# The second mixer's stages in another order: stick-breaking first, the recurrence last

## Chip, cores and metric

One Trainium2 chip, one core. The metric is the device time of one launch in microseconds (us); a change of some 0.2% can be told from none.

## What is computed

Two transformer blocks follow each other on 512 tokens of width 1024, in fp32. The first has a hybrid mixer, cross attention and a feed-forward part; the second has two layers of feed-forward, **mixer**, feed-forward, each with a modulated norm. The change lies in that mixer alone, which runs twice:

```python
def _mixer(h, ...):
    (lru_x, lru_g, sb_q, sb_k, sb_v, fx_q, fx_k, fx_v, fx_f) = split(h @ w_in)
    u = causal_depthwise_conv(lru_x, conv_w, conv_b)
    y_lru = rg_lru(u, w_rgate, b_rgate, w_igate, b_igate, lru_lambda) * gelu(lru_g)
    y_sb = stick_breaking_attention(sb_q, sb_k, sb_v)
    fq, fk = rms(fx_q) * g_qk[0], rms(fx_k) * g_qk[1]
    log_f = log_sigmoid(fx_f + b_fgate)
    y_fox = forgetting_attention(fq, fk, fx_v, log_f)
    y = concat([rms(y_lru), rms(y_sb), rms(y_fox)]) * g_mix_out
    return y @ w_out
```

The recurrence `rg_lru` has two block-diagonal gates with a sigmoid, a decay `a = exp(log_a)`, a factor `sqrt(1 - a*a)` and a scan over the 512 tokens. The stick-breaking attention weighs a key by its own log-sigmoid plus a reversed running sum over later keys; the forgetting attention is a softmax with a decay from cumulated forget gates. Each has four heads of 64; the recurrence is 512 wide.

## The kernel before

**Tiles.** Activations are kept with features on the partitions, 128 x 512 tokens a tile. Every large product is made of three fp32r matmuls (`mm3`, L343: high x high, high x low, low x high), so each weight tile (128 x 1024, DMA on SP's queue, `weights` L329) is split by ACT (`wh`) and by DVE or POOL (`wl`). There are 3 raw, 6 high and 6 low weight buffers, 43 activation buffers ("a"), 12 rotating ones ("r"), 3 PSUM buffers "mm" for the large products and 5 "x" for all else.

**Order.** TensorE's order is written by hand. `Flow` (L209) keeps a planned time: the main generator yields the planned TensorE time of each product, and side streams (spawned with a delay) are run whenever their planned time has come, ahead of the main one. A side stream that must let another engine work yields `Wait`. The delays are the constants in `T` (L193): `lru_sum` 25.0, `rsqrt` 3.51, `fqk` 8.0, `fox` 1.0, `fox_1` 0.9, `fox_2` 0.41, `stick` 1.81, `stick_l` 4.0, `finish` 4.91. TensorE then executes in this fixed order and waits wherever an input is late. The other engines are ordered by the framework's scheduler, by program order among what is ready.

**The mixer** (`mixer2`, L1322), main stream in this order:

1. `dense_t` of eight feature tiles, the first five "ahead" in token halves while the norm before is still made: gelu branch `lgg` (4), then the convolved branch `lx` (4, four DVE operations each, L1336 and L1339).
2. `lru` (L1268) is spawned: eight gate matmuls `lg` (L1281) with weights `bd`, tanh, exp, sqrt on ACT, products on POOL, scans on DVE (L1305), times gelu, sum of squares; then the function table 6 (exp and ln) is loaded and, 25 planned us later, the norm (`spread`: column sums `ms`, inverse root, row broadcast `bc`) makes `HL`.
3. `dense_tok` of the forgetting queries and keys (`fqk`), normed per head and turned (`turn`, 8 us later, into `FT`).
4. `dense_t` of the forget gate, then `gates` (L1384): transposes, log-sigmoid, cumulated sums `cs`, four row broadcasts `fb`.
5. `dense_t` of the stick queries and keys (`sqk`).
6. The streams `stick(t)` and `fox(t)` for the four query blocks t = 0 to 3 of 128 tokens are spawned; `heads` (L993) chains the blocks of a kind. A stick needs all scores, Abs, Exp, Ln, a reversed scan, a POOL subtraction and an Exp before its transposes and products; a forgetting block runs its four heads through `pipeline` (L1062). Each block ends with `finish` (norm and turn into `YT`).
7. `dense_tok` of the values `v`, beside 6.
8. `slab4` with the first half of `w_out` on the recurrence's `HL` (96 matmuls), then `end_plain` with the second half on `YT`, by token halves, where `made` waits for the blocks of a half.

Of the kernel before, what the change touches and what calls it, by code (L numbers as in the profile page):

```python
# [19 lines left out]
S = 512  # L20
# [262 lines left out]
class Core:  # L283
# [706 lines left out]
        yield from self.end_post(I["w_out"][0], AT, Y, "post_mix_g", self.nxt1("pre_mem_g"), H2,  # L990
                                 self.rows_apart, lambda hf: _joined([halves[hf]]))

    def heads(self, makers, delay, opened=None):  # L993


        out = []

        def chain(i):
            if i and opened is None:
                yield from _joined([out[i - 1]])  # L1000
            elif i:
                yield from _joined(out[:i - 1])
                while i - 1 not in opened or opened[i - 1] > self.flow.t:
                    yield Wait(0.5)
            yield from makers[i]()
        for i in range(len(makers)):
            out.append(self.flow.spawn(chain(i), delay))
        return out
# [256 lines left out]
                                        op0=OP.mult)  # L1265
            self.a4.append(a4), self.hb.append(hb)

    def lru(self, l, LX, LG, HL):  # L1268

        nc, I = self.nc, self.I  # L1270
# [4 lines left out]
        U, R, G, sums = [], [], [], []  # L1275
        for m in range(4):
            u = LX[m]
            r, g = self.act("lr"), self.act("li")
            for q, o in enumerate((r, g)):
                ps = self.ps("x", "lg")  # L1280
                nc.tensor.matmul(ps, bd[q][:, m * 128:m * 128 + 128], u,  # L1281
                                 start=True, stop=True)
                nc.scalar.activation(o, ps, AF.Tanh, scale=0.5, bias=hb[:, q * 4 + m:q * 4 + m + 1])
                yield _pe(512)
            nc.vector.scalar_tensor_tensor(u, g, 1.0, u, op0=OP.add, op1=OP.mult)

            nc.scalar.activation(g, r, AF.Tanh, scale=a4[:, m:m + 1], bias=a4[:, m:m + 1])
            U.append(u), R.append(r), G.append(g)
        bd.clear()
        yield Wait(T["lru_tanh"])  # L1290
        for m in range(4):
            c = a4[:, 4 + m:5 + m]
            nc.scalar.activation(R[m], R[m], AF.Exp, scale=c, bias=c)
        for m in range(4):
            u, a, g = U[m], R[m], G[m]

            q = self.rot("a2")
            nc.gpsimd.tensor_tensor(q, a, a, op=OP.mult)
            nc.vector.scalar_tensor_tensor(g, q, 1.0, g, op0=OP.add, op1=OP.mult)
        for m in range(4):  # L1300
            u, a, g = U[m], R[m], G[m]
            nc.scalar.activation(g, g, AF.Sqrt, scale=0.25)
            nc.gpsimd.tensor_tensor(u, u, g, op=OP.mult)
            hs = self.rot("hs")
            nc.vector.tensor_tensor_scan(hs, a, u, 0.0, op0=OP.mult, op1=OP.add)  # L1305
            nc.vector.tensor_tensor(u, hs, LG[m], op=OP.mult)
            self.square_sum(sums, u, self.rot)

        self.table = self.load_table(6)
        yield Wait(T["lru_sum"])  # L1310
        out = []
        yield from self.spread(sums, 4, 1.0 / 512, out)
        for m in range(4):
            t = self.rot("ln")
            nc.vector.scalar_tensor_tensor(t, U[m], self.vec(f"g_mix{l}", m), out[0], op0=OP.mult,
                                           op1=OP.mult)
            hi, lo = self.act("lh", F32R), self.act("ll", F32R)
            nc.scalar.activation(hi, t, AF.Copy)
            nc.vector.tensor_tensor(lo, t, hi.bitcast(F32), op=OP.subtract)
            HL.append((hi, lo))  # L1320

    def mixer2(self, l, H, H2):  # L1322
        nc, I, flow = self.nc, self.I, self.flow
        LX, LG, Q, K, v = {}, {}, {}, {}, {}


        cw = lambda j, m: self.vec(f"conv_w{l}", j * 4 + m)

        def lru_in(i, ps):
            if i < 4:  # L1330
                LG[i] = self.act("lgg")
                nc.scalar.activation(LG[i], ps, AF.Gelu_apprx_tanh)
            else:
                i -= 4
                u = self.act("lx")
                nc.vector.tensor_scalar(u, ps, cw(3, i), self.vec(f"conv_b{l}", i), op0=OP.mult,  # L1336
                                        op1=OP.add)
                for d in (1, 2, 3):
                    nc.vector.scalar_tensor_tensor(u[:, d:], ps[:, :S - d], cw(3 - d, i), u[:, d:],  # L1339
                                                   op0=OP.mult, op1=OP.add)  # L1340
                LX[i] = u
        yield from self.dense_t([I["m_t"][l, i] for i in (4, 5, 6, 7, 0, 1, 2, 3)], H, lru_in, 5)
        HL, self.table, self.calm = [], None, False
        lru = flow.spawn(self.lru(l, LX, LG, HL), 1.0)


        fqk, FT, squares = {}, [], {}
# [1 line left out]
        def qk(t, ps):  # L1349
# [27 lines left out]
        fT = self.rot("fT")  # L1377

        def gate_in(i, ps):
            nc.scalar.activation(fT[:4], ps[:4], AF.Copy)  # L1380
        yield from self.dense_t([I["m_f"][l]], H, gate_in)
        NF, FB = self.tp.tile([128, 16], F32, tag="nf", bufs=1, name=self.nm("NF")), []

        def gates():  # L1384
# [30 lines left out]
                FB.append(o)  # L1415
                yield 4 * _pe(128)
        gated = flow.spawn(gates(), 1.0)

        def qk_stick(i, ps):
            d = self.act("sqk")  # L1420
            if i < 2:
                nc.scalar.activation(d, ps, AF.Copy, scale=0.125)
                Q[i] = d
            else:
                nc.vector.tensor_copy(d, ps)
                K[i - 2] = d
# [49 lines left out]
        def fox(t):  # L1476
# [10 lines left out]
            def score(h):  # L1487
                if h % 2 == 0:
                    scs[h], scs[h + 1] = scores(FT[:2], FT[2:], h // 2, t, self.mask["le"])
                sc = scs.pop(h)  # L1490
                e = es[h] = self.rot("fe")
                nc.vector.tensor_tensor_reduce(out=e[:, :n], in0=sc, in1=FB[h][:, :n], scale=1.0,
                                               scalar=-3.0e38, op0=OP.add, op1=OP.max,
                                               accum_out=m[:, h:h + 1])
                c = slice(h, h + 1)
                nc.vector.tensor_tensor(b[:, c], nf[:, c], m[:, c], op=OP.subtract)
                nc.vector.tensor_tensor(b[:, c], b[:, c], nf[:, c], op=OP.subtract)
                nc.scalar.activation(e[:, :n], e[:, :n], AF.Exp, bias=b[:, c],
                                     accum_out=lsum[:, c])
                return 0.0 if h % 2 else _pe(n) + 0.2  # L1500

            def second(h):
# [12 lines left out]
        def stick(t):  # L1515
# [52 lines left out]
        yield from self.dense_tok([I["m_v"][l, c] for c in range(4)], H, keep, e=nc.gpsimd)  # L1568
        H.clear()
# [12 lines left out]
        yield from self.end_plain(I["m_o"][l, 1], YT, gate, self.nxt2(l, 2), H2, made)  # L1582


    def program(self, stop):
# [77 lines left out]
```

## Time and profile before

| what | us |
|---|---|
| median of 3 runs | 2888.01 (2886.16 to 2888.03) |
| the profiled execution | 2887.57 |
| its span | 2885.5 |
| busy in it: TensorE / DVE / ACT / POOL | 2784.1 / 1534.0 / 1027.6 / 383.5 |
| mean granted TensorE clock | 0.98 |

All times in the rows are from one profiled execution. A TensorE that is busy is one with a matmul in it; the ends of matmuls are modelled, so the spacing of starts tells its rate better. In a row of waits the releaser is the engine, tile and line that came last. In a row of stretches the numbers in brackets are instructions.

### The profile page before, as it was taken

The page shows a single profiled execution, that of the slowest core. Times are in us where ns is not written, and L with a number is a line of the kernel's source. Part 1 is how long each engine was busy: PE and PEld are TensorE (multiplying, and loading weights), DVE is VectorE, ACT ScalarE, POOL GpSimd, SP SyncE. Part 2 cuts the span into 40 slices and gives each one's busy share as a digit, 9 for nine tenths or more (in the row PEclk, how much of TensorE's full clock was granted, in tenths as well). Part 3 has the DMA queues.
Part 4 walks back from the last instruction along what each step waited for, and adds up shares of the span by engine and source line. Part 5 has one row for each costly group of instructions (what it writes and reads, how often), then busy time and mean ns, then how long its engine had stood idle before and what let it go on. Part 6 is the DMA issues. An engine that isn't in the chain of part 4 may idle for free. (4 is left out here: it accounts for less than half of the span.)

```text
span 2885.5 us, 36900 instructions
## 1 busy us (share of the span) xinstructions
PE 2784.1 (96%) x14492; PEld 2355.3 (82%) x14492; DVE 1534.0 (53%) x2931; ACT 1027.6 (36%) x1725; POOL 383.5 (13%) x376
## 2 busy tenths in 40 slices
PE   8999998999989999998799999999999988999999
PEld 7888878888878888887588888888888875888888
DVE  6465666645456444466766454463333667643333
ACT  4355444323233222245543222342222535432221
POOL 3010303101032000024310000110000232200000
PEclk9999999999998999999999999999999997999999
DMA  5322322555433555431115555353332321133322
GB/s 164 121 69 88 103 88 74 168 160 169 148 114 123 160 169 161 139 116 54 52 52 162 156 174 159 112 173 110 102 95 88 95 62 34 52 98 93 102 90 71
DMA packets 94606, 326.07 MB, mean 113 GB/s; under 512 B 11232, under 2 KB 15584, under 8 KB 94432
## 3 DMA queue, kind: packets, MB, share of 16 engines
q1 hardware_dynamic: 94288, 323.53, 36.4%
q8 instruction: 114, 1.87, 0.3%
q14 instruction: 60, 0.49, 0.1%
q10 hardware_dynamic: 144, 0.18, 0.0%
HBM read 321.37 MB, written 2.10 MB: 112 GB/s over the span
## 5 line engine op out<-in xcount | busy, mean ns | idle before, releaser
L338 ACT ACTIVATE wh<-wr 128x1024 fp32r<-128x1024 f32 x456 | 482.3, 1060 | 1273.0 <-PE mm L347 494.8
L346 PE MATMUL mm<-hh,wh 128*128 128x512 f32 (+1 forms) x2344 | 856.9, 366 | 7.3 <-ACT fqk L1352 2.4
L348 PE MATMUL mm<-hh,wl 128*128 128x512 f32 (+1 forms) x2344 | 852.4, 364 | 3.0 <-DVE wl L340 3.0
L347 PE MATMUL mm<-hl,wh 128*128 128x512 f32 (+1 forms) x2344 | 852.9, 364 | 1.7 <-DVE hl L500 1.6
L340 DVE TENSOR_TENSOR wl<-wr,wh 128x1024 fp32r<-128x1024 f32 x440 | 541.8, 1233 | 343.1 <-ACT wh L338 341.2
L346 PEld LDWEIGHTS mm<-hh,wh 128*128 128x128 f32 x2344 | 448.4, 191 | 76.6 <-ACT fqk L1352 3.3
L348 PEld LDWEIGHTS mm<-hh,wl 128*128 128x128 f32 x2344 | 448.4, 191 | 71.2 <-DVE wl L340 3.6
L347 PEld LDWEIGHTS mm<-hl,wh 128*128 128x128 f32 x2344 | 448.2, 191 | 69.6 <-DVE hl L500 2.0
L795 DVE CUSTOM_DVE_ANT_0 ada<-ada,c 128x1024 f32<-128x1024 f32 x144 | 180.4, 1253 | 314.4 <-DMA ada<-in_w_ada_dram 314.2
L346 PE MATMUL dn<-uh,wh 128*128 128x512 f32 x720 | 280.1, 389 | 0.0
L347 PE MATMUL dn<-ul,wh 128*128 128x512 f32 x720 | 280.1, 389 | 0.0
L348 PE MATMUL dn<-uh,wl 128*128 128x512 f32 x720 | 280.1, 389 | 0.0
L490 POOL TENSOR_TENSOR acc<-sq,sq 128x256 f32<-128x256 f32 (+1 forms) x34 | 38.3, 1129 | 1377.2 <-ACT sq L487 1377.2
L633 DVE TENSOR_TENSOR sg<-mm,sg 128x512 f32<-128x512 f32 x110 | 75.9, 690 | 181.8 <-PE mm L348 177.4
L346 PE MATMUL mmt<-wh,hh 128*128 128x512 f32 x352 | 147.1, 418 | 12.1 <-ACT wh L338 8.2
L348 PEld LDWEIGHTS dn<-uh,wl 128*128 128x128 f32 x720 | 135.1, 188 | 28.1
L346 PEld LDWEIGHTS dn<-uh,wh 128*128 128x128 f32 x720 | 135.1, 188 | 28.1
L347 PEld LDWEIGHTS dn<-ul,wh 128*128 128x128 f32 x720 | 135.1, 188 | 28.0
L347 PE MATMUL mmt<-wl,hh 128*128 128x512 f32 x352 | 141.3, 402 | 0.5 <-DVE wl L340 0.5
L348 PE MATMUL mmt<-wh,hl 128*128 128x512 f32 x352 | 141.4, 402 | 0.0
L490 POOL TENSOR_TENSOR acc<-acc,sq 128x256 f32<-128x256 f32 (+1 forms) x140 | 122.5, 875 | 72.5 <-ACT sq L487 57.3
L669 DVE SCALAR_TENSOR_TENSOR X<-dn,gate,X 128x512 f32<-128x512 f32 x64 | 48.0, 750 | 155.6 <-PE dn L348 155.6
(322 smaller groups left out, 3611.1 us busy)
## 6 DMA issues: line engine op xcount, KB each, us to landing
wr<-in_f_gu_dram SPq DMA_DIRECT2D x176, 512.0 KB, 3.6
ada<-in_w_ada_dram SPq DMA_DIRECT2D x144, 512.0 KB, 4.2
wr<-in_f_dn_dram SPq DMA_DIRECT2D x88, 512.0 KB, 3.5
wr<-in_w_gu_dram SPq DMA_DIRECT2D x44, 512.0 KB, 3.6
wr<-in_w_in_dram SPq DMA_DIRECT2D x28, 512.0 KB, 3.5
wr<-in_m_t_dram SPq DMA_DIRECT2D x24, 512.0 KB, 3.5
wr<-in_w_dn_dram SPq DMA_DIRECT2D x22, 512.0 KB, 4.0
wr<-in_m_v_dram SPq DMA_DIRECT2D x16, 512.0 KB, 3.5
```

What stands on the lines that cost most here:

```text
L338: nc.scalar.activation(hi, raw, AF.Copy)
L340: (e or nc.vector).tensor_tensor(lo, raw, hi.bitcast(F32), op=OP.subtract)
L346: mm(ps, ah, bh, start=start, stop=False)
L347: mm(ps, ah, bl, start=False, stop=False)
L348: mm(ps, al, bh, start=False, stop=stop)
L490: nc.gpsimd.tensor_tensor(acc, accs.pop(), sq, op=OP.add)
L633: nc.vector.tensor_tensor(t, ps, t, op=OP.mult)
L669: self.nc.vector.scalar_tensor_tensor(self.X[m], ps, gate(m), self.X[m], op0=OP.mult, op1=OP.add)
L795: nc.vector.tensor_tensor_reduce(out=w, in0=w, in1=c, scale=1.0, scalar=0.0, op0=OP.mult, op1=OP.add, accum_out=ml[:, i:i + 1])
```

## The change

The mixer's main stream has another order: first the five tiles of the stick queries and keys and of the forget gate (now the "ahead" ones), then the function table 6, `gates` and the sticks, the values, the forgetting queries and keys with `turn` and the forgetting heads, and only then the eight tiles of the recurrence, convolved branch first. Query blocks run from t = 3 down to 0. The attention's half of `w_out` comes before the recurrence's, which is now the last product, by token halves. `lru` waits until the last exponential of the last forgetting block (`opened["last"]`) is issued and keeps its tanh behind it on ACT; gelu is applied at its end; the norm is made in two token halves, the second of which may follow later. The constants in `T` are not changed; `lru_tanh` and `lru_end` are no longer used.

```diff
-    def heads(self, makers, delay, opened=None):
+    def heads(self, makers, delay, opened=None, top=None):
...
-                while i - 1 not in opened or opened[i - 1] > self.flow.t:
+                at = i - 1 if top is None else top - (i - 1)
+                while at not in opened or opened[at] > self.flow.t:
                     yield Wait(0.5)
...
-    def lru(self, l, LX, LG, HL):
+    def lru(self, l, LX, LG, HL, opened):
...
+        while "last" not in opened:
+            yield Wait(0.5)
         bd = [self.act("bd") for _ in range(2)]
...
         for m in range(4):
+            while len(LX) <= m:
+                yield Wait(0.5)
             u = LX[m]
...
-                nc.scalar.activation(o, ps, AF.Tanh, scale=0.5, bias=hb[:, q * 4 + m:q * 4 + m + 1])
+                with self.tc.issue_after(opened["last"]):
+                    nc.scalar.activation(o, ps, AF.Tanh, scale=0.5,
+                                         bias=hb[:, q * 4 + m:q * 4 + m + 1])
                 yield _pe(512)
...
-        yield Wait(T["lru_tanh"])
...
-            hs = self.rot("hs")
-            nc.vector.tensor_tensor_scan(hs, a, u, 0.0, op0=OP.mult, op1=OP.add)
-            nc.vector.tensor_tensor(u, hs, LG[m], op=OP.mult)
-            self.square_sum(sums, u, self.rot)
-
-        self.table = self.load_table(6)
+            nc.vector.tensor_tensor_scan(g, a, u, 0.0, op0=OP.mult, op1=OP.add)
+        while len(LG) < 4:
+            yield Wait(0.5)
+        sums = []
+        for m in range(4):
+            nc.scalar.activation(LG[m], LG[m], AF.Gelu_apprx_tanh)
+            nc.vector.tensor_tensor(U[m], G[m], LG[m], op=OP.mult)
+            self.square_sum(sums, U[m], self.rot)
+        HL += [(self.act("lh", F32R), self.act("ll", F32R)) for _ in range(4)]
+
+        def norm(hf):
+            sl, out = slice(hf * 256, hf * 256 + 256), []
+            yield from self.spread([sums[0][:, sl]], 2, 1.0 / 512, out)
+            for m in range(4):
+                t = self.half("ln")
...
         yield Wait(T["lru_sum"])
-        out = []
-        yield from self.spread(sums, 4, 1.0 / 512, out)
...
+        yield from norm(0)
+        opened["half"] = flow.t
+        yield from norm(1)
 
     def mixer2(self, l, H, H2):
...
-        yield from self.dense_t([I["m_t"][l, i] for i in (4, 5, 6, 7, 0, 1, 2, 3)], H, lru_in, 5)
-        HL, self.table, self.calm = [], None, False
-        lru = flow.spawn(self.lru(l, LX, LG, HL), 1.0)
+        yield from self.dense_t([I["m_t"][l, 8 + i] for i in range(4)] + [I["m_f"][l]], H, entry, 5)
+        self.calm = False
+
+        self.table = self.load_table(6)
...
-        yield from self.dense_tok([I["m_v"][l, 4 + c] for c in range(4)], H, qk)
...
-        turned = flow.spawn(self.turn(fqk, "fT", FT, scaled), T["fqk"])
...
-        yield from self.dense_t([I["m_f"][l]], H, gate_in)
...
-        yield from self.dense_t([I["m_t"][l, 8 + i] for i in range(4)], H, qk_stick)
...
+                last = nc.scalar.activation(e[:, :n], e[:, :n], AF.Exp, bias=b[:, c],
+                                            accum_out=lsum[:, c])
+                if (t, h) == (0, 3):
+                    opened["last"] = last.ins
...
-        sticks = self.heads([lambda t=t: stick(t) for t in range(4)], T["stick"], opened)
-        new_y(2, 3)
-        foxes = self.heads([lambda t=t: fox(t) for t in range(4)], T["fox"])
+        sticks = self.heads([lambda t=t: stick(t) for t in (3, 2, 1, 0)], T["stick"], opened, 3)
...
         yield from self.dense_tok([I["m_v"][l, c] for c in range(4)], H, keep, e=nc.gpsimd)
+        yield from self.dense_tok([I["m_v"][l, 4 + c] for c in range(4)], H, qk)
+        turned = flow.spawn(self.turn(fqk, "fT", FT, scaled), T["fqk"])
+        new_y(2, 3)
+        foxes = self.heads([lambda t=t: fox(t) for t in (3, 2, 1, 0)], T["fox"])
...
+        lru = flow.spawn(self.lru(l, LX, LG, HL, opened), 1.0)
+        yield from self.dense_t([I["m_t"][l, i] for i in range(8)], H, lru_in)
         H.clear()
...
-        yield lru
-        yield Wait(T["lru_end"])
-        yield from self.slab4(I["m_o"][l, 0], HL, ev, e=nc.gpsimd)
+        yield from _joined(sticks + foxes)
+        yield from _joined(list(ends.values()))
+        yield from self.slab4(I["m_o"][l, 1], [YT[k] for k in range(4)], ev, e=nc.gpsimd)
+        YT.clear()
+
         def made(hf):
-            ts = (2 * hf, 2 * hf + 1)
-            yield from _joined([q[t] for q in (sticks, foxes) for t in ts])
-            yield from _joined([ends[y0, t] for y0 in (0, 2) for t in ts])
+            if hf == 0:
+                while "half" not in opened:
+                    yield Wait(0.5)
+            else:
+                yield from _joined([lru])
         self.modulated(3 * l + 3)
-        yield from self.end_plain(I["m_o"][l, 1], YT, gate, self.nxt2(l, 2), H2, made)
+        yield from self.end_plain(I["m_o"][l, 0], HL, gate, self.nxt2(l, 2), H2, made)
```

## Rows read from the trace of the kernel before

**Rows 1.** first part of the page: engine, busy us, share of the span, instructions
```profile
PE 2784.1 (96%) x14492; PEld 2355.3 (82%) x14492; DVE 1534.0 (53%) x2931; ACT 1027.6 (36%) x1725; POOL 383.5 (13%) x376
```

**Rows 2.** busy time by stretch: start:end, us, engines, PEclk, DMA share, GB/s
```profile
1245.00:1486.00 241.00, 215.36 (x1219) 173.41 (x1218) 168.01 (x421) 119.50 (x252) 65.11 (x48) 0.96 0.22 68
2242.00:2493.60 251.60, 227.33 (x1234) 183.04 (x1233) 166.18 (x416) 121.51 (x256) 62.98 (x48) 0.91 0.19 59
```

**Rows 3.** TensorE's waits, 1272 to 1376: waiter, releaser, us, times, longest
```profile
PE f L1387 <- ACT fT L1380: 2.4, 1, 2.4
PE tp L684 <- POOL fqk L1364: 2.0, 1, 2.0
PE mmt L346 <- ACT fqk L1352: 1.5, 1, 1.5
PE mm L346 <- ACT fqk L1352: 1.2, 1, 1.2
PE cs L1401 <- DVE ls_r L1245: 0.5, 1, 0.5
```

**Rows 4.** TensorE's waits in layer 1, 2240 to 2530
```profile
PE tp L684 <- ACT fe L1498: 7.2, 5, 3.5
PE cs L1401 <- DVE rs_a L452: 4.0, 1, 4.0
```

**Rows 5.** busy time by stretch, attention part of layer 0
```profile
1374.00:1437.00 63.00, 49.20 (x267) 34.98 (x265) 48.81 (x137) 38.51 (x108) 23.76 (x19) 0.89 0.12 36
1437.00:1476.00 39.00, 36.40 (x255) 29.99 (x255) 26.37 (x109) 16.75 (x46) 0.00 (x0) 1.00 0.11 38
1476.00:1486.00 10.00, 10.00 (x47) 8.23 (x46) 6.47 (x17) 1.92 (x4) 0.00 (x0) 1.00 0.35 104
```

**Rows 6.** TensorE's waits, attention part of layer 0, 1376 to 1486
```profile
PE tp L684 <- ACT fe L1498: 4.1, 5, 1.5
PE FO L1455 <- ACT pT L326: 2.7, 1, 2.7
PE S L1439 <- ACT ab L1528: 2.4, 2, 1.8
...
PE SO L1455 <- ACT pT L326: 1.5, 1, 1.5
```

**Rows 7.** TensorE's timeline: start us, us, line, operation (gates; two token matmuls)
```profile
1294.97 7.34 PE L1281 MATMUL lg<-lx,bd 128*128 128x512 f32 x16
...
1371.67 0.39 PE L346 MATMUL mmt<-wh,hh 128*128 128x512 f32 x1
1371.89 0.39 PE L347 MATMUL mmt<-wl,hh 128*128 128x512 f32 x1
```

**Rows 8.** DVE's groups by shape, 1273 to 1300: busy us, mean ns
```profile
L1339 DVE SCALAR_TENSOR_TENSOR lx<-mm,V,lx 128x510 f32<-128x510 f32 x4 | 3.0, 747 | 0.1
```

**Rows 9.** the tile bd (block weights of the gates): its load
```profile
DMA to landing us min/median/max: 4.0/4.3/4.4
```

**Rows 10.** ACT's timeline: a table load and the activation behind it
```profile
1300.75 1.28 ACT L1293 ACT_TABLE_LOAD   x1
1302.04 0.82 ACT L1293 ACTIVATE lr<-lr,a 128x512 f32<-128x512 f32 x1
```

**Rows 11.** POOL's timeline: the recurrence's last sum of squares
```profile
1327.40 1.42 POOL L490 TENSOR_TENSOR acc<-acc,sq 128x512 f32<-128x512 f32 x1 [2.68 <-ACT sq L487]
```

**Rows 12.** DVE's timeline: first and last of eleven operations of an inverse root
```profile
1414.58 0.14 DVE L447 TENSOR_SCALAR rs_m<-fs 128x1 f32<-128x1 f32 x1
...
1416.47 0.16 DVE L453 SCALAR_TENSOR_TENSOR rs_y<-rs_a,rs_y 128x1 f32<-128x1 f32 x1
```

**Rows 13.** the tile bc: half rows of a norm, ns min/median/max
```profile
L515 DVE SCALAR_TENSOR_TENSOR hn<-X,G,bc x32: 468/473/481, 1243.1 to 1526.2; 128x256 f32<-128x256 f32 x32
```

**Rows 14.** TensorE's timeline behind its longest wait of layer 0
```profile
1428.17 0.72 PE L1455 MATMUL FO<-v,pT 128*128 128x64 f32 x4 [2.71 <-ACT pT L326]
```

**Rows 15.** busy time by stretch, four us later (PEclk behind the POOL column)
```profile
1432.00:1436.00 4.00, 4.00 (x14) 3.38 (x14) 3.56 (x6) 2.18 (x3) 1.28 (x1) 0.57 0.00 0
```

More of the change, by code (lines that the diff above doesn't have):

```diff
@@ L1266, in lru_consts @@
             self.a4.append(a4), self.hb.append(hb)
-    def lru(self, l, LX, LG, HL):
-        nc, I = self.nc, self.I
+    def lru(self, l, LX, LG, HL, opened):
+        nc, I, flow = self.nc, self.I, self.flow
+        while "last" not in opened:
+            yield Wait(0.5)
         bd = [self.act("bd") for _ in range(2)]
@@ L1274, in lru @@
         a4, hb = self.a4[l], self.hb[l]
-        U, R, G, sums = [], [], [], []
+        U, R, G = [], [], []
         for m in range(4):
+            while len(LX) <= m:
+                yield Wait(0.5)
             u = LX[m]
@@ L1303, in lru @@
             nc.gpsimd.tensor_tensor(u, u, g, op=OP.mult)
-            hs = self.rot("hs")
-            nc.vector.tensor_tensor_scan(hs, a, u, 0.0, op0=OP.mult, op1=OP.add)
-            nc.vector.tensor_tensor(u, hs, LG[m], op=OP.mult)
-            self.square_sum(sums, u, self.rot)
-        self.table = self.load_table(6)
-        yield Wait(T["lru_sum"])
-        out = []
-        yield from self.spread(sums, 4, 1.0 / 512, out)
[L1313 to L1320, printed above, removed]
+            nc.vector.tensor_tensor_scan(g, a, u, 0.0, op0=OP.mult, op1=OP.add)
@@ new lines, in lru @@
+        while len(LG) < 4:
[11 more added lines that the diff above has]
+                t = self.half("ln")
+                nc.vector.scalar_tensor_tensor(t, U[m][:, sl], self.vec(f"g_mix{l}", m), out[0],
+                                               op0=OP.mult, op1=OP.mult)
+                hi, lo = HL[m][0][:, sl], HL[m][1][:, sl]
+                nc.scalar.activation(hi, t, AF.Copy)
+                nc.vector.tensor_tensor(lo, t, hi.bitcast(F32), op=OP.subtract)
@@ L1322, in mixer2 @@
+        yield Wait(T["lru_sum"])
+        yield from norm(0)
+        opened["half"] = flow.t
+        yield from norm(1)
     def mixer2(self, l, H, H2):
         nc, I, flow = self.nc, self.I, self.flow
[L1324 to L1332, printed above, removed]
-            else:
[L1334 to L1341, printed above, removed]
@@ L1342, in mixer2, with entry @@
-        yield from self.dense_t([I["m_t"][l, i] for i in (4, 5, 6, 7, 0, 1, 2, 3)], H, lru_in, 5)
-        HL, self.table, self.calm = [], None, False
-        lru = flow.spawn(self.lru(l, LX, LG, HL), 1.0)
+        Q, K, v = {}, {}, {}
+        fT = self.rot("fT")
+        def entry(i, ps):
+            if i == 4:
+                nc.scalar.activation(fT[:4], ps[:4], AF.Copy)
+                return
+            d = self.act("sqk")
+            if i < 2:
+                nc.scalar.activation(d, ps, AF.Copy, scale=0.125)
+                Q[i] = d
+            else:
+                nc.vector.tensor_copy(d, ps)
+                K[i - 2] = d
@@ L1373, in scaled @@
                 nc.vector.tensor_scalar(o, ps, self.vec(f"g_k{l}"), None, op0=OP.mult)
-        turned = flow.spawn(self.turn(fqk, "fT", FT, scaled), T["fqk"])
-        fT = self.rot("fT")
-        def gate_in(i, ps):
-            nc.scalar.activation(fT[:4], ps[:4], AF.Copy)
-        yield from self.dense_t([I["m_f"][l]], H, gate_in)
         NF, FB = self.tp.tile([128, 16], F32, tag="nf", bufs=1, name=self.nm("NF")), []
@@ L1417, in mixer2 @@
         gated = flow.spawn(gates(), 1.0)
[L1419 to L1426, printed above, removed]
-        yield from self.dense_t([I["m_t"][l, 8 + i] for i in range(4)], H, qk_stick)
         YT = {}
@@ L1497, in score @@
                 nc.vector.tensor_tensor(b[:, c], b[:, c], nf[:, c], op=OP.subtract)
-                nc.scalar.activation(e[:, :n], e[:, :n], AF.Exp, bias=b[:, c],
-                                     accum_out=lsum[:, c])
+                last = nc.scalar.activation(e[:, :n], e[:, :n], AF.Exp, bias=b[:, c],
+                                            accum_out=lsum[:, c])
+                if (t, h) == (0, 3):
+                    opened["last"] = last.ins
                 return 0.0 if h % 2 else _pe(n) + 0.2
@@ L1568, in mixer2, with lru_in @@
         yield from self.dense_tok([I["m_v"][l, c] for c in range(4)], H, keep, e=nc.gpsimd)
+        yield from self.dense_tok([I["m_v"][l, 4 + c] for c in range(4)], H, qk)
+        turned = flow.spawn(self.turn(fqk, "fT", FT, scaled), T["fqk"])
+        new_y(2, 3)
+        foxes = self.heads([lambda t=t: fox(t) for t in (3, 2, 1, 0)], T["fox"])
+        LX, LG, HL = {}, {}, []
+        cw = lambda j, m: self.vec(f"conv_w{l}", j * 4 + m)
+        def lru_in(i, ps):
+            if i < 4:
+                u = self.act("lx")
+                nc.vector.tensor_scalar(u, ps, cw(3, i), self.vec(f"conv_b{l}", i), op0=OP.mult,
+                                        op1=OP.add)
+                for d in (1, 2, 3):
+                    nc.vector.scalar_tensor_tensor(u[:, d:], ps[:, :S - d], cw(3 - d, i), u[:, d:],
+                                                   op0=OP.mult, op1=OP.add)
+                LX[i] = u
+            else:
+                LG[i - 4] = self.act("lgg")
+                self.copy(i, LG[i - 4], ps)
+        lru = flow.spawn(self.lru(l, LX, LG, HL, opened), 1.0)
+        yield from self.dense_t([I["m_t"][l, i] for i in range(8)], H, lru_in)
         H.clear()
@@ L1573, in ev @@
             nc.vector.scalar_tensor_tensor(self.X[m], ps, gate(m), self.X[m], op0=OP.mult, op1=OP.add)
[L1574 to L1576 removed]
+        yield from _joined(sticks + foxes)
+        yield from _joined(list(ends.values()))
+        yield from self.slab4(I["m_o"][l, 1], [YT[k] for k in range(4)], ev, e=nc.gpsimd)
+        YT.clear()
         def made(hf):
[L1578 to L1580 removed]
+            if hf == 0:
+                while "half" not in opened:
+                    yield Wait(0.5)
+            else:
+                yield from _joined([lru])
         self.modulated(3 * l + 3)
[L1582 removed]
+        yield from self.end_plain(I["m_o"][l, 0], HL, gate, self.nxt2(l, 2), H2, made)
     def program(self, stop):
```

## The prediction

> **What bounds the kernel now.** I read the page's first part first. TensorE is busy for 96% of the span [rows 1], and no other engine comes near. An edit that takes no matmul off TensorE can therefore win only TensorE's idle time or its slow clock. The reader should next look at the two stretches in which the second mixer runs, once in each layer, from its first projection matmul to the first matmul of its last product [rows 2]. They last 241.0 and 251.6 us, with 215.36 and 227.33 us of TensorE in them: idle 25.6 and 24.3 us. The granted clock is a mean of 0.96 and 0.91, so the missing clock is worth at most 0.04 x 241 = 9.6 and 0.09 x 251.6 = 22.6 us. Without both, the layers hold 205.8 and 204.7 us of work. That they agree to 1 us says that this accounting is sound: each layer has some 205 us of work, and an excess of 35.2 and 46.9 us, **82.1 us together**. That is all the change can act on.
>
> Where the excess lies is read from TensorE's waits. In the projection part of layer 0 [rows 3] five rows add to 7.6 us: gate transposes wait for the copy of their input (2.4), transposes of the forgetting keys and queries for POOL (2.0), two accumulators that are handed on late (1.5 and 1.2), and the gates' sums (0.5; 4.0 in layer 1 [rows 4]). The attention part holds more [rows 5]: where sticks and forgetting heads run together, DVE is busy 48.81 of 63 us, TensorE idles 63 - 49.20 = 13.8 us and its clock is 0.89; the next 39 us idle 2.6. Its waits are small and many [rows 6]: transposes wait for the forgetting exponentials (4.1), forgetting products for a copy (2.7), stick scores for a PSUM buffer that ACT still reads (2.4), stick products for a copy (1.5), and so on. The remaining 25.6 - 7.6 - 16.4 = 1.6 us lie at the head of the mixer. The last 10 us before the mixer's last product are full [rows 5]: the recurrence's product lies there as cover for the end of the attention.
>
> **The change, part by part.** No matmul is added or removed; the norm of the recurrence is only split in two halves. So the 205 us stay, and I sum the new excess per layer.
>
> *Head and gates.* The head keeps its 1.6 us. The gate projection is now the fifth of the first five tiles, still followed after a planned 1 us by its transposes. Its copy stands behind two more copies on ACT, while the planned 1 us is unchanged: 0 to 2.4 us [rows 3], I take 1.5. The gates' sums wait for a row of some twenty small DVE operations, which now share DVE with the first stick: 0.5 to 4.0 [rows 3, 4], I take 1.5.
>
> *Accumulator hand-overs.* A token-wise projection holds two of three "mm" buffers at a time, so each change of pair waits for a copy. The rows of before are 1.5 and 1.2 us [rows 3]. After the change values and forgetting projections follow each other directly, four hand-overs at some 1.1: 4.5 us; 0 if ready attention steps fall in between.
>
> *Sticks.* They run under values and forgetting projections, 2 x 96 matmuls of 0.227 us [rows 7] = 43.6 us of filler, without the forgetting heads beside them. What waited on them before (2.4 for scores, 1.5 for products [rows 6]) came while ACT and DVE had both kinds in their queues. I take 2 us of 3.9; bounds 0 and 3.9.
>
> *Turning the forgetting keys.* It waited 2.0 us for POOL [rows 3]. Now the first forgetting score is due half a planned us behind the last transpose and needs its copy, on a DVE that has convolutions queued: 0 to 3, I take 1.5.
>
> *Forgetting heads.* They run under the recurrence's eight tiles, 192 x 0.227 = 43.6 us. By the planner's delays (about 9 us until they start, then 14.5, 12.5, 11 and 5.5 us to the last exponential of block 0, in which they take some 17 us of TensorE) the main stream gets about 35 of its planned 41 us in, so the filler just lasts. The price is DVE: each convolution is four operations of some 0.75 us [rows 8], four of them 12 us, in front of the score reductions. Of before's 4.1 + 2.7 us [rows 6] (7.2 instead of 4.1 in layer 1 [rows 4]) I keep 5 us; bounds 2 and 10.
>
> *Start of the recurrence.* It may only be issued after the last forgetting exponential. Its eight gate matmuls stand at once in TensorE's queue, behind them the rest of the recurrence's projection. They run some 6.8 us (7.34 with the overlap of the last [rows 7]), but they wait for the block weights, whose load takes 4.3 us [rows 9] and needs two of 43 activation buffers. At that point the code holds 16 (H), 4 (v), 4 (decay rows), 8 (outputs), 4 (turned keys), 4 (convolutions) and 2 or 3 of the gelu branch, so the load starts when the decay rows fall free, perhaps 4 us ahead. They also need the tanh table (1.28 us [rows 10]) before ACT frees their PSUM: 0 to 5, I take 3.
>
> *Tail.* This is what the change adds. From the last exponential, TensorE has 3 + 6.8 us for the gates, about 2 us of attention, some 7 us of projection left over and 96 x 0.227 = 21.8 us of the attention's product: about 41 us. The recurrence needs 3.5 us to its first tanh; before, it took from 1294.97 (first gate matmul) to 1327.40 + 1.42 (last sum of squares) [rows 7, 11], 33.9 us; the gelu's table and the later product add some 1 to 3 us: about 39 us. So it fits, barely. But the planner sets the norm's first matmul 25 us (T lru_sum) behind the gelu step, and that product is planned at 20.5 us. So in TensorE's fixed order the norm stands behind the whole product, with nothing after it but what waits for it. The gap is the inverse root (2.05 us from first to last of its eleven operations [rows 12]), the two small matmuls with their hand-overs (about 1.2), the first split (half a row 0.47 [rows 13], two more such steps on ACT and DVE: about 1.4) and another 1 to 1.5 for the next three, which come slower than the 0.34 us in which TensorE uses one (three half matmuls, 3 x 0.227 / 2): 6 us, an estimate, not below 4.5. Before, this wait was hidden under the values.
>
> Idle: 1.6 + 1.5 + 1.5 + 4.5 + 2 + 1.5 + 5 + 3 + 6 = **26.6 us** per layer, against 25.6 and 24.3: nothing is won there. The win is the clock. At 1428 TensorE had waited 2.71 us, the longest gap of layer 0, and four us later it still ran at a granted clock of 0.57, so mostly at the lower of its two levels (1.2 of 2.4 GHz) [rows 14, 15]. The gaps of the attention become shorter and lie in denser work, so I take 5 us of loss there and 3 behind the tail's gap: 8 us, bounds 4 and 16, against 9.6 and 22.6.
>
> Sum: 34.6 us per layer, 69.2 for both, against 82.1: **12.9 us faster**. The profiled execution took 2887.57 us, its span 2885.5 plus 2.1 around it; the median is 2888.01, practically the same. 2888 - 12.9 = **2875 us**.
>
> ACT's switches of function table are priced here at 1.28 us, and the next activation starts 1.29 us after the load began [rows 10]. The Trainium skill ("ScalarE: Activation LUTs", What ACT_TABLE_LOAD costs) puts a drain of some 1.38 us behind each load, 2.66 us in all. By that, an estimate, the tail's three switches would end it 4.1 us later, and the sum would be some 2881; the row shows no such drain, so it isn't used.
>
> **Rivals.** *The recurrence becomes the bound of the mixer's end* (slower). If the filler is used up before the last exponential, the 7 us of projection are gone. The cover is then 3 + 6.8 + 21.8 = 31.6 us against a chain of up to 3.5 + 33.9 + 3 = 40.4 us: 8.8 us more of waiting and some 3 more of slow clock, 46.4 per layer, 93 in all: 2888 + 11 = 2899. The same would happen if sqrt and gelu alternate on ACT, since nothing orders them and each switch is 1.28 us. It decides from 82.1 / 2 - 34.6 = 6.4 us per layer on. For it: the chain fits by 2 us only. Against it: DVE is emptier than at 1310 to 1328, where the chain was measured.
>
> *The attention is covered wholly.* With twice the filler beside it, hand-overs, heads and sticks cost 3 instead of 11.5 us and the clock 5: 23.1 per layer, 46 in all, 2888 - 36 = 2852. For it: at 1437 to 1476, DVE less loaded, only 2.6 us idle and clock 1.00 [rows 5]. Against it: the order on TensorE is fixed by planned times, and the delays are unchanged.
>
> *An even trade.* Tail and recurrence start cost 12 instead of 9 and the clock 11: 40.6 per layer, 81.2 in all, 2887.
>
> **How the numbers follow.** A measurement of this kernel can tell about 0.2%, 5.8 us, from no change. Forecast (2866 to 2882): 0.43. Wholly covered (2852): 0.13. Even trade: 0.16. Tail bound (2894 to 2905): 0.28. So faster 0.56, same 0.16, slower 0.28. The range leaves out half of the covered case and the worse third of the tail's: 2856 to 2901.
>
> **What would show it.** Right: two mixer stretches of about 240 us each, alike; no wait above 2 us in the stick part; a mean clock of 0.97; one wait of 4 to 7 us of the norm's matmuls or the last product in each layer. Wrong: waits for the sum of squares or for the splits over 12 us (tail bound), forgetting transposes waiting more than before's 4.1 and 7.2 us (DVE under the convolutions), or layer 1 at a low clock again without long gaps.

## The result and the profile after

The changed kernel took **2928.61 us** (median of 4 runs, 2924.08 to 2929.86), the kernel before 2887.9 beside it: a ratio of 1.014, 95% interval 1.0122 to 1.0157, or some 41 us slower. Forecast were 2875, with a range of 2856 to 2901.

The first part of the page after, the line that answers to [rows 1]: engine, busy us, share of the span, instructions.

```profile
PE 2783.2 (95%) x14492; PEld 2360.2 (81%) x14492; DVE 1540.9 (53%) x2973; ACT 1033.7 (35%) x1739; POOL 382.2 (13%) x376
```

TensorE runs as many matmuls, and is busy for 2783.2 us against 2784.1. The span, 2928.1 us, is 42.6 us longer, so on balance what came is idle time. Busy time by stretch shows where: for the kernel after, the two mixer stretches from the first projection matmul to the first of the last product, then the two last products (start:end, length, busy us of PE, PEld, DVE, ACT, POOL with instruction counts, PE's granted clock, DMA share, GB/s).

```profile
1245.70:1509.10 263.40, 215.93 (x1214) 176.75 (x1212) 165.45 (x415) 120.92 (x253) 62.99 (x48) 0.91 0.19 59
2270.55:2532.50 261.95, 217.00 (x1214) 175.66 (x1212) 164.27 (x413) 121.22 (x253) 63.11 (x48) 0.91 0.18 57
...
1509.10:1537.58 28.48, 27.79 (x206) 27.28 (x207) 20.19 (x59) 12.49 (x28) 10.95 (x12) 0.89 0.15 42
2532.50:2561.20 28.70, 28.03 (x206) 27.52 (x207) 19.68 (x57) 12.43 (x28) 10.65 (x12) 0.88 0.13 38
```

The same view of the kernel before, with the second stretch cut at its first projection matmul (in [rows 2] it begins 1.9 us earlier), and its last products:

```profile
1245.20:1486.35 241.15, 215.51 (x1218) 173.50 (x1217) 167.81 (x420) 119.41 (x252) 64.92 (x48) 0.96 0.22 68
2243.90:2493.65 249.75, 225.48 (x1218) 181.19 (x1218) 164.52 (x414) 119.88 (x251) 62.54 (x48) 0.90 0.19 58
...
1486.35:1511.25 24.90, 24.34 (x203) 24.12 (x202) 15.57 (x34) 10.79 (x22) 10.64 (x12) 1.00 0.20 65
2493.65:2518.55 24.90, 24.33 (x203) 24.09 (x202) 15.54 (x34) 10.79 (x22) 10.62 (x12) 1.00 0.22 64
```

The stretches grew by 22.3 and 12.2 us and the last products, now run behind a wait and at first at a low clock, by 3.6 and 3.8: 41.8 of 42.6 us. In the stretches TensorE idles 47.5 and 45.0 us instead of 25.6 and 24.3. Its waits in the stretch of layer 0, then of layer 1 (waiter, releaser, us, times, longest), answer to [rows 3, 4, 6]:

```profile
PE tp L684 <- DVE fy L1463: 18.4, 2, 16.7
PE cs L1409 <- DVE ls_r L1246: 12.7, 1, 12.7
PE bc L476 <- DVE rs_y L453: 3.5, 1, 3.5
PE tp L684 <- ACT fe L1496: 2.7, 3, 1.4
PE tp L684 <- DVE fb L1494: 2.7, 1, 2.7
...
PE f L1395 <- ACT fT L1347: 1.4, 1, 1.4
PE mmt L346 <- ACT v L1566: 1.2, 1, 1.2
```

```profile
PE tp L684 <- DVE fy L1463: 18.1, 2, 16.4
PE cs L1409 <- DVE ls_r L1246: 11.0, 1, 11.0
```

Two single waits make up 29.4 and 27.4 us, more than the 21.9 and 20.7 us by which the idle time grew; the rest got shorter. **The gates' sums** (`cs`): the DVE timeline of layer 0 with the two engines beside it (start, us, engine, line, operation, shape, [idle before <- releaser]):

```profile
1287.68 0.68 DVE L1526 COPY z<-S 128x512 f32<-128x512 f32 x1
1288.28 0.16 DVE L1233 TENSOR_TENSOR lp_p<-lp_p,lp_q 128x16 f32<-128x16 f32 x1
...
1291.39 0.68 DVE L1536 SCALAR_TENSOR_TENSOR ab<-z,ab 128x512 f32<-128x512 f32 x1
1291.99 1.28 DVE L1234 TENSOR_SCALAR lp_p<-lp_p 128x16 f32<-128x16 f32 x1
1293.18 1.21 DVE L1538 TENSOR_TENSOR_SCAN ab<-ones,ab 128x512 f32<-128x512 f32 x1
1294.32 0.14 DVE L1233 TENSOR_TENSOR lp_p<-lp_p,lp_q 128x16 f32<-128x16 f32 x1
...
1302.37 0.18 DVE L1246 TENSOR_TENSOR ls_r<-ls_r,lp_p 128x16 f32<-128x16 f32 x1
```

```profile
1291.48 1.75 POOL L1540 TENSOR_TENSOR z<-z,ab 128x512 f32<-128x512 f32 x1 [9.74 <-DVE lp_p L1233]
```

```profile
1302.70 0.56 PE L1409 MATMUL cs<-ls_r,tri 128*128 128x4 f32 x2 [12.74 <-DVE ls_r L1246]
```

The log-sigmoid of the gates is a row of 22 instructions of some 0.17 us, nearly all dependent on the one before. Between them stand twelve of the first stick's, 0.6 to 1.2 us each, 10.3 us in all. Four of the small ones take 1.25 to 1.28 us and end when a GpSimd operation ends. So the row lasts from 1285.7 to 1302.5. TensorE's order is fixed, and behind the sums stand value matmuls that could have run.

**The last forgetting block's finish** (`fy`): ACT, then DVE, then TensorE of the kernel after, at the end of layer 0's attention.

```profile
1444.43 0.67 ACT L1291 ACTIVATE lr<-lg,hb 128x512 f32<-128x512 f32 x1
...
1459.48 0.63 ACT L1310 ACTIVATE li<-li 128x512 f32<-128x512 f32 x1 [0.97 <-DVE li L1307]
1460.02 0.35 ACT L499 ACTIVATE yh<-tp,V 128x128 fp32r<-128x128 f32 x1
1460.27 0.40 ACT L1460 ACTIVATE fsq<-fo 128x256 f32<-128x256 f32 x1
```

```profile
1459.37 7.67 DVE L1313 TENSOR_TENSOR_SCAN li<-lr,lx 128x512 f32<-128x512 f32 x4
...
1467.21 0.14 DVE L447 TENSOR_SCALAR rs_m<-fs 128x1 f32<-128x1 f32 x1
...
1471.83 1.43 DVE L1463 TENSOR_SCALAR fy<-fo,rs_y 128x256 f32<-128x256 f32 x1
```

```profile
1456.30 0.39 PE L348 MATMUL mm<-hh,wl 128*128 128x512 f32 x1
1473.41 0.66 PE L684 MATMUL tp<-ident,fy 128*128 128x128 f32 x2 [16.73 <-DVE fy L1463]
```

The recurrence may start behind the last forgetting *exponential*. But that block still has its products, its square (L1460), inverse root and scale (L1463) to come. They are issued after the recurrence, and stand behind its tanh, exponentials and square roots on ACT and its four scans on DVE. TensorE has the block's transposes ahead of what was left of the projection, and waits 16.73 us.

Two lines of GpSimd belong to it, sums of the recurrence's squares:

```profile
1471.85 1.26 POOL L490 TENSOR_TENSOR acc<-acc,sq 128x512 f32<-128x512 f32 x1
1484.84 1.30 POOL L490 TENSOR_TENSOR acc<-acc,sq 128x512 f32<-128x512 f32 x1 [11.72 <-issue]
```

The first runs beside the scale `fy`, which took 1.43 us where that of the block before had taken 0.35 (at 1444.44); a step of the root ahead of it (1470.57) took 1.23 in place of 0.16, beside another such sum. That is some 2.2 of the 16.73 us; no run tests it. The second is the recurrence's last sum of squares.

### The profile page after: what moved, and what is told of

The parts are those of the page before. It is cut to its first block, busy times and chain, and to the rows that moved or that the text cites. A ratio compares the mean times of both kernels' runs of the same rounds, so it can differ in the third digit from the quotient of the medians.

```text
span 2928.1 us, 36992 instructions
## 1 busy us (share of the span) xinstructions
PE 2783.2 (95%) x14492; PEld 2360.2 (81%) x14492; DVE 1540.9 (53%) x2973; ACT 1033.7 (35%) x1739; POOL 382.2 (13%) x376
## 4 chain that ended last, share of the span: by engine, by line
PE 84%; DVE 10%; ACT 3%; POOL 2%; issue 1%; DMA 1%; POOLq 0%; ACTq 0%; DVEq 0%
PE mm L346 15%; PE mm L348 15%; PE mm L347 15%; PE dn L348 6%; PE dn L346 6%; PE dn L347 6%; PE mmt L346 2%; PE mmt L347 2%; PE mmt L348 2%; PE slh L347 2%; PE slh L346 2%; PE slh L348 2%; PE tp L684 1%; DVE wl L340 1%; PE sl L347 1%
```

## The experiments

The kernel before took 2891 us beside all of them; by its ratio the changed kernel stands at 2932 there. Three theories went in. A, **queue order**: what TensorE waits for stands behind work that isn't urgent. B, **capacity**: DVE is full. C, **the recurrence's chain** sets the mixer's end (the prediction's rival).

| kernel | us | ratio to before (95%) | gain on the change |
|---|---|---|---|
| changed | 2928.6 | 1.014 (1.0122 to 1.0157) | |
| e10_sub_on_dve | 2925.8 | 1.0119 (1.0102 to 1.0136) | 6 |
| e1_gate_later | 2917.9 | 1.0094 (1.0079 to 1.0109) | 13 |
| e2_finish_first | 2917.2 | 1.0091 (1.0076 to 1.0106) | 14 |
| e8_short_series | 2901.4 | 1.0040 (1.0025 to 1.0055) | 29 |
| e3_both | 2900.9 | 1.0036 (1.0023 to 1.0049) | 30 |
| e4_both_norm_early | 2898.2 | 1.0023 (1.0013 to 1.0032) | 34 |
| e6_sums_apart | 2891.4 | 1.0004 (0.9994 to 1.0013) | 39 |
| e9_all_norm_late | 2876.2 | 0.9953 (0.9936 to 0.9970) | 54 |
| e5_scan_after_split | 2875.8 | 0.9953 (0.9938 to 0.9968) | 54 |
| e7_all | 2869.7 | 0.9931 (0.9916 to 0.9946) | 60 |

The last column is the difference of the ratios times 2891. It is uncertain by some 6 to 7 us in each row, most of it shared by all of them, so e10's 6 us aren't clear of noise by time alone.

**e1: the sums later in TensorE's order.**

```diff
-gate_f=6.0
+gate_f=20.0
```

> Only the planned wait ahead of the gates' cumulated sums is longer (T gate_f 20 instead of 6), so that their matmuls stand some 14 planned us later in TensorE's order; DVE's work is untouched. Theory A (queue order: the changed kernel is slower because TensorE stands in its fixed order behind small DVE chains that DVE has mixed with or put behind larger work): the waits of 12.7 and 11.0 us for the log-sigmoid go, and most of the slow clock behind them; about 2897 us (2888 to 2905). Theory B (DVE is short of capacity in this order, the wait comes back at the sticks' or the forgetting heads' steps): 2912 or more, with new waits of 8 us or more per layer for DVE or ACT.

2917.9: A's range (2888 to 2905) is missed, and the time is within B's, though the new wait is below the 8 us that B asked for. The wait for `ls_r` is gone from the list, but half of it came back one step on. TensorE's wait of layer 0:

```profile
PE fb L1418 <- DVE NF L1411: 5.7, 1, 5.7
```

The broadcast (`fb`) is planned 0.6 us behind the sums and needs a copy of them (`NF`), which now stands on DVE behind the second stick's scans and two weight splits.

**e2: the recurrence behind the last block's scale.**

```diff
 lru:
-        while "last" not in opened:
+        while "end" not in opened:
 finish, after the scale:
+            if (y0, t) == (2, 0):
+                opened["end"] = flow.t
```

> The recurrence's stream starts only after the last forgetting block has issued its closing square, inverse root and scaling, so these stand ahead of the recurrence on ACT and DVE. Theory A (queue order): the waits of 16.7 and 16.4 us for fy go, the projection tiles run meanwhile; the recurrence starts some 4 us later; about 2893 us (2885 to 2905). Theory C (the recurrence's chain from the last forgetting exponential sets the end of the mixer in any case): the wait moves to the norm's sums or the split, 8 us or more per layer; 2908 or more.

Again half: A's 2893 is missed, and this is what C had asked for, in time (2908 or more) and in the place of the new wait. TensorE's waits of e2, layer 0:

```profile
PE sl L347 <- DVE yl L500: 8.0, 2, 6.4
PE bc L476 <- DVE rs_y L453: 3.5, 1, 3.5
PE sl L346 <- ACT yh L499: 3.0, 1, 3.0
...
PE tp L684 <- DVE fy L1463: 1.7, 1, 1.7
```

`fy` fell from 18.4 to 1.7 us, and 11 us appeared at the block's next step, the split into `yh` and `yl`, which is planned 4.91 us later and so issued behind the recurrence again.

**e3 and e4: both moves; then also the norm planned earlier** (e4).

```diff
-lru_sum=25.0
+lru_sum=18.0                                    # e4
```

> Both edits, the later gate sums and the recurrence behind the last block's closing steps. Theory A: the gains add, about 2862 us (2852 to 2874), faster than the kernel before. Theories B or C: 2885 or more, the new order costs the same elsewhere.

> Both edits, and the planned delay ahead of the recurrence's norm is 18 instead of 25 us, so its column sums and row broadcast stand inside the attention's product and not behind it. Theory A, and the prediction's tail term (6 us per layer for a norm with nothing beside it): 8 to 12 us below the kernel with both edits, about 2852. Theory C: the sum of squares isn't ready then, TensorE waits for it inside the product, no gain or slower than the kernel with both edits.

The gains of e1 and e2 add (13 + 14, measured 30), but A's 2862 is missed by 39 us, and 2900.9 is where B and C (2885 or more) had it. The trace of e3, layer 0, shows it isn't C: DVE, then TensorE.

```profile
1455.85 7.68 DVE L1313 TENSOR_TENSOR_SCAN li<-lr,lx 128x512 f32<-128x512 f32 x4
1463.45 0.32 DVE L500 SCALAR_TENSOR_TENSOR yl<-tp,V,yh 128x128 fp32r<-128x128 f32 x1
```

```profile
1463.82 0.80 PE L347 MATMUL sl<-yl,wh 128*128 128x512 f32 x1 [6.13 <-DVE yl L500]
...
1491.98 1.23 PE L476 MATMUL bc<-ident,rs_y 128*128 128x128 f32 x4 [3.48 <-DVE rs_y L453]
```

What is late is the attention's split behind the scans; the recurrence's norm costs 3.48 us, as planned. The earlier norm alone (e4) brought about 3 us more, where A had 8 to 12.

**e5, e6, e7: the next step of each chain freed as well**, on top of e4: square roots, scans and gelu behind the split (e5), the broadcast 8 us behind the sums (e6), both (e7).

```diff
 lru, ahead of the square roots:                 # e5, e7
+        while "fin" not in opened:              # set behind the split
+            yield Wait(0.5)
-gate_s=0.6
+gate_s=8.0                                      # e6, e7
```

> Edit, on top of both moves and the earlier norm: the recurrence's square roots, scans and gelu are also issued behind the split of the last forgetting block, not only its tanh behind that block's scale. In the trace of both moves the split of the last block stood behind a square root that waited for its input (first product of the attention's half waits 3.0 us for yh), and behind the four scans of 7.68 us and the gate products (6.1 and 1.6 us for yl): 10.7 us in the first layer, 10.9 in the second. Theory A (queue order): these waits fall to about 1 us a layer, the scans begin at the same time as before, since their inputs were the last to come; with the clock's part 22 to 26 us less than the run of both moves with the earlier norm, so about 2873 us where the kernel before takes 2889. Theory B (VectorE is short of capacity): what the split gains the scans and the norm lose, at most 6 us less, 2890 or more. Theory C (the recurrence's chain sets the mixer's end): the wait for the split goes but comes back in front of the last product as a wait for lh or rs_y of 8 us or more a layer; about 2890.

> Edit, on top of both moves and the earlier norm, without the change to the recurrence's scans: TensorE's planned distance between the gates' running sums and the broadcast of their copy is 8 us in place of 0.6. With the sums moved later, TensorE waited 5.7 us a layer for the copy NF of the sums, which stood on VectorE behind two weight splits of 3.88 us and the second stick's scans. Theory A (queue order): that wait goes and nothing comes in its place; with the clock's part 11 to 16 us less than the run of both moves with the earlier norm, about 2884 us. Theory B (VectorE short of capacity): the later broadcasts meet a VectorE and ScalarE that are full, the wait moves to the sticks' outputs or to the broadcast's copies, at most 4 us less, 2892 or more. Theory C says nothing of this run: it expects what A does or less.

> Edit: all of these together (sums later and apart from their broadcast, last forgetting block's scale and split ahead of the recurrence's tanh and scans, norm planned 7 us earlier). Theory A (queue order): the gains add, 33 to 42 us less than the run of both moves with the earlier norm: about 2860 us, faster than the kernel before by 1%. What is then left of the second mixer's excess should be near the sum of the prediction. Theory B (VectorE short of capacity): 2885 or more. Theory C (the recurrence's chain sets the mixer's end): the gates' part is gained and the split's is not, about 2882, with a wait of 8 us or more a layer ahead of the last product.

e5 took 20 us off by the ratios (22 by the medians; A had 22 to 26), and left B and C (2890 or so) far off. In e7 the split runs before the scans (DVE), and the last product starts 29 us earlier than after the plain change (TensorE):

```profile
1452.29 0.34 DVE L500 SCALAR_TENSOR_TENSOR yl<-tp,V,yh 128x128 fp32r<-128x128 f32 x1
...
1453.75 0.34 DVE L500 SCALAR_TENSOR_TENSOR yl<-tp,V,yh 128x128 fp32r<-128x128 f32 x1
1454.41 2.30 DVE L1315 TENSOR_TENSOR_SCAN li<-lr,lx 128x512 f32<-128x512 f32 x1 [0.32 <-POOL lx L1313]
```

```profile
1480.01 0.39 PE L346 MATMUL slh<-lh,wh 128*128 128x256 f32 x1 [1.02 <-ACT lh L1333]
```

e6 gained only 5 us by the ratios (7 by the medians), between A (11 to 16) and B (at most 4). The wait of 11.3 us for `NF` is gone from both layers, but waits for `v` rose from 2.8 to 5.9 and waits for `yl` (2.7) and for the sticks' copies appeared, as B had said. That the engines are too full in that stretch is argued from these waits, not shown. e7 beats the kernel before by 0.7%; A's 2860 is missed by 10 us, while B and C (2882 and more) are missed by 12 and more. Busy time of its two mixer stretches:

```profile
1245.80:1480.00 234.20, 211.14 (x1214) 170.00 (x1212) 160.07 (x415) 123.90 (x255) 65.94 (x48) 0.98 0.21 64
2240.40:2472.80 232.40, 209.85 (x1217) 168.35 (x1215) 159.78 (x414) 124.07 (x256) 66.28 (x48) 0.99 0.20 62
```

Idle 23.1 and 22.6 us, at a clock of 0.98 and 0.99.

**e8: six of the series' seven steps left out**, nothing else.

```diff
-            for d in (13, 11, 9, 7, 5, 3, 1):
+            for d in (1,):                        # gates only
```

> Edit, on the changed kernel with nothing else: the log-sigmoid of the gates sums one term of its series in place of seven, so 12 of its some 20 instructions on VectorE (128x16 each) are left out in each layer, and the gates are slightly off. All else, TensorE's order too, is as in the changed kernel. Theory A (queue order: the series is long because its steps alternate one by one with the first stick's instructions of 0.7 to 1.3 us): the gates' sums find their input within 1 us in place of 12.7 and 11.0 us, and TensorE's wait in front of them all but goes; 22 to 33 us less than the changed kernel, 2898 to 2909 us. Theory B (VectorE is short of capacity in this stretch): the series' own work is some 2 to 3 us a layer, so the wait falls by no more than that and the rest comes back at the first sticks' outputs: 2920 or more.

29 us, within A's 22 to 33. The wait is gone in both layers without any other order: in e8 the sums start at once, with no idle in front.

```profile
1289.51 0.28 PE L1409 MATMUL cs<-ls_r,tri 128*128 128x4 f32 x2
```

The twelve instructions left out are worth 2 us of DVE by their own durations; in the queue they cost TensorE 12.7 and 11.0. e8 takes out both what lengthens the row, the stick's instructions between and GpSimd's hold; e10 below takes out the second alone.

**e9: e7 with the norm at the changed kernel's place.**

```diff
-lru_sum=18.0
+lru_sum=25.0
```

> Edit: the version with all moves, but with the norm of the recurrence planned at the changed kernel's 25 us again, so that its sums stand behind the whole product of the attention's half. Theory A (queue order): the tail is then as long as the prediction had it (root, broadcast and split behind the product: waits of 3.5 and 0.4 us and the small products between them), 4 to 8 us more than with the earlier norm, 2874 to 2878 us. Theory C (the recurrence's chain sets the mixer's end): the squares are then late either way and the norm's place changes less than 2 us, about 2870.

6.5 us slower than e7, within A's 4 to 8, though by the ratios (6 us) no more than their noise. The traces agree. The broadcast of the norm in layer 0, in e7, then in e9:

```profile
1477.94 0.71 PE L476 MATMUL bc<-ident,rs_y 128*128 128x128 f32 x4 [0.99 <-DVE rs_y L453]
```

```profile
1481.01 0.71 PE L476 MATMUL bc<-ident,rs_y 128*128 128x128 f32 x4 [3.48 <-DVE rs_y L453]
```

**e10: the first stick's subtractions on DVE in place of GpSimd.**

```diff
-nc.gpsimd.tensor_tensor(Z[h], Z[h], L[h], op=OP.subtract)
+(nc.vector if t == 3 else nc.gpsimd).tensor_tensor(Z[h], Z[h], L[h], op=OP.subtract)
```

> Edit, on the changed kernel with nothing else: the subtraction that follows each scan of the first stick (block 3, four times 128x512) runs on VectorE in place of GpSimd. In the changed kernel four of the log-sigmoid's TENSOR_SCALARs (128x16) took 1.25 to 1.28 us in place of 0.17, each time until a subtraction on GpSimd that had begun before them was over. If the GpSimd operation holds them, they fall to 0.17 us, 4.3 us less in the row of the gates, and four subtractions of some 0.69 us stand in the same row in their place: the sums wait some 1.6 us less than 12.7 and 11.0, and the kernel takes 2 to 5 us less than the changed kernel, 2925 to 2930 us. If their length has another reason, they stay at 1.25 us, the wait grows to some 15 us a layer, and the kernel takes 5 us more or so, 2936 us.

6 us faster by the ratios, as much as their noise; the traces decide. With the subtractions off GpSimd none of the series' instructions takes over 0.18 us, though DVE has four more of 0.69 us in the same row. TensorE's wait fell from 12.7 and 11.0 to 8.7 and 8.6 us. DVE and TensorE of e10:

```profile
1291.39 0.15 DVE L1234 TENSOR_SCALAR lp_p<-lp_p 128x16 f32<-128x16 f32 x1
...
1292.13 0.69 DVE L1540 TENSOR_TENSOR z<-z,ab 128x512 f32<-128x512 f32 x1
1292.74 0.17 DVE L1234 TENSOR_SCALAR lp_p<-lp_p 128x16 f32<-128x16 f32 x1
```

```profile
1297.77 0.56 PE L1409 MATMUL cs<-ls_r,tri 128*128 128x4 f32 x2 [8.68 <-DVE ls_r L1246]
```

## Why the prediction was wrong, step by step

- **What bounds the kernel, and that only idle time and clock can change**: right. The work stayed, and the layers became alike (263.4 and 262.0).
- **The finish of the last forgetting block: not in the sum.** This is the step that failed most: 16.7 and 16.4 us against nothing. The part on the recurrence's start asked what its gate matmuls would wait for, and the tail asked whether its chain fits under TensorE's filler. Neither asked who stands *behind* the recurrence on ACT and DVE. e2 and e5 together show the mechanism: issued ahead, the scale and then the split end these waits.
- **Gates' sums: 1.5 us, bounds 0.5 and 4.0; measured 12.7 and 11.0.** That the row now shares DVE with the first stick stood in the text; the price was still that of rows where it didn't. Its 16.8 us are the twelve of the stick's between (10.3), what GpSimd held four of its own for (4.4), and the small ones themselves. e8 shows that its length in the queue is the cause, and e10 that at least 4.0 us of layer 0's wait (12.7 to 8.7) hung on GpSimd's operations.
- **Tail: 6 us.** From the sum's matmuls (1502.91) to the last product (1509.14) it was 6.2. Right, and e9 shows that an earlier place takes some 3 us a layer off it.
- **Clock: 16 us to be won (32.2 to 16); measured about 1.** The step multiplied the missing clock by the whole stretch, idle time included, where it costs nothing: in the two long waits of layer 0 (1290.00 to 1302.70 and 1456.50 to 1473.50) the granted clock was 0.63 and 0.62 with hardly a matmul in them. By TensorE's busy time layer 1 won 8.5 us (225.48 to 217.00) and layer 0 lost 0.4, while the last products, outside the stretches, lost 3.5 and 3.7, about the 3 us forecast behind the tail's gap. That both layers came to 205 us was thus no proof of the method: by it the kernel after would have 263.4 x 0.91 - 47.5 = 192 us of work. It was chance too: the stretch of layer 1 in [rows 2] began 1.9 us early, and cut at the first projection matmul it gives 249.75 x 0.90 - 24.3 = 200.5.
- **Other terms**: accumulator hand-overs 4.5, measured 1.2; sticks 2, measured 1.4 (0.8 + 0.3 + 0.3); turning the keys 1.5 and the recurrence's start 3, each single wait 0.5 or less (no table load stands ahead of the first tanh at 1444.43); gate transposes 1.5, measured 1.4; forgetting heads 5, measured 2.7 + 2.7 (4.8 in layer 1). Together they came out too dear, which hid some of the miss.
- **The rival "the recurrence becomes the bound"** had the sign, not the mechanism. From its first gate matmul (1440.35) to its last sum of squares (1484.84 + 1.30) the recurrence took 45.8 us, longer than the 33.9 of before, since its last gelu tile came from the projection that TensorE held back behind `fy` (copied at 1481.35). It was still done 16.8 us before its norm's sums (1502.91), which waited for nothing. e5 and e7 took the wait of the split away, and the norm still found its sums in time: in e7 the chain took 33.6 us (1437.98 to 1471.55) and was done 3.4 us ahead. Once nothing held the projection back, the term of 33.9 and the narrow fit came out.
- **Function tables**: a load at 1461.26 took 1.28 us and the next activation began 1.29 us after it, as in [rows 10]. The drain that the Trainium skill ("ScalarE: Activation LUTs", What ACT_TABLE_LOAD costs) puts behind a load shows in none of these rows. The 2881 that the prediction gives by that page doesn't follow from its own terms: 4.1 us in each layer make 2883, or 2879 where the 2 us by which the chain fits are used up first, both estimates. The tail had two loads (1455.55 and 1461.26), not three.

The sum was made for a kernel in which nothing urgent stands behind the recurrence or the stick. e9, which keeps the tail where the prediction had it, comes closest to that one: 26.6 us of idle forecast per layer, 23.7 and 24.8 measured; 12.9 us faster than the kernel before forecast, 13.6 measured by its ratio. That the last figure fits so well is luck in part, as the clock's part was reckoned by a method that fails and single terms were off both ways. The order itself was worth something; the issue order on DVE and ACT, which the change left to program order, took it back and more.

What stays open: how much of e6's missing gain is DVE's load and how much the order on ACT; no run parts them. Nor does one tell what GpSimd's sums beside the last block's scale cost.

## What to carry to other kernels

When a side chain is moved to a new place, list on each engine that works off a queue not only what the chain waits for but what will be queued behind it, and whether the busiest engine has that next in its fixed order. Price a row of small dependent instructions by the long ones that it will alternate with, not by its own durations. When a move returns half of what it should, look one dependent step further along the same chain before giving up the theory: here every second half lay there.

## What the runs showed of the hardware

A DVE instruction of 128x16 that takes 0.17 us took 1.28 when it began (1291.99) inside a GpSimd subtraction (1291.48 to 1293.23): it ended at 1293.27, with it. All eight such instructions of the two layers fell back to 0.18 or less when the subtraction was moved (e10). Others in the two layers show the same without a test: a root's step of 128x1 (0.16 us) took 1.23 at 1470.57 and at 2493.45, each beside a GpSimd sum. The Trainium skill ("SBUF — State Buffer", Who interferes with whom) says that the two engines share a port pair, and that in the cases it lists, `tensor_scalar` in a two-port mode among them, the one that issues first holds it for its whole instruction while the other fully blocks. The trace agrees, at 1.1 us for each, though no row shows in which mode the small instructions ran.
